# The last row blocks of a hybrid decoder layer: residual added ahead of a plain store, gates into tiles of their own, squares ahead of scalings

## The chip, the core and the metric

The kernel runs on one NeuronCore of a Trainium2 chip. Five engines work side by side, each with its own queue that it runs strictly in order: PE (TensorE) multiplies matrices into PSUM banks, DVE (VectorE) and ACT (ScalarE) work on tiles of 128 partitions, POOL (GpSimd) does the same more slowly and also issues DMAs, and SP (SyncE) issues DMAs. An instruction waits on semaphores of the instructions whose data it needs, and everything behind it in its queue waits with it. The metric is the device time of one execution in microseconds (us).

## The reference

One decoder layer on `x` of 1024 rows by 1024 columns in float32. Only its last line matters here:

```python
        h = rmsnorm(x, pre_w_mlp[l]) * (1.0 + sc2) + sh2
        u = jnp.square(jax.nn.relu(h @ w_up[l]))
        x = x + g2 * rmsnorm(u @ w_down[l], post_w_mlp[l])
    return x
```

So each row of the product `u @ w_down` is squared and summed over its 1024 columns, scaled by the inverse root of that mean, multiplied by `g2 * post_w_mlp` (in the kernel `gw2`, the gate), and added to the residual `x`.

## The kernel before

The output is cut into eight row blocks `tb` of 128 rows and two column halves of 512. The tile `accs[tb][half]` in SBUF, written (tb, half) below, gathers the product of the down projection. That projection is done by Strassen's scheme: seven products `n` instead of eight for each pair of row blocks t and t + 4, over five groups of the inner dimension (`GROUPS`). Each product of the last group (`g` = 4, two inner pairs `p`) is `dmm`: 2 x 3 matmuls of 128x128 by 512 columns, since every float32 operand is split into a high and a low part. Some products share a PSUM bank and go on summing in it, and `accum` on DVE adds the bank's running sum to a tile after each of them (`PLAN`): a, the bank of products 1, 6, 7 and 4; c, of 5 and 3; b, of 2. So within one bank each product has to wait until DVE has read the sum of the one before.

In the last group the order of work is a hand-written list of 24 steps (`order`, line 1586), three row pairs interleaved and the first three products of the fourth pair behind them. All five engine queues are pinned (class `Queue`): the instructions of each stand in exactly the order in which the code issues them. A step issues its matmuls, then the `accum` of the product of the step before, and then what the dictionary `later` holds for this step, in the order in which it was put there. The steps that matter, with the tile that each product is added to:

| step | product, bank | added to | step | product, bank | added to |
|---|---|---|---|---|---|
| 16 | 4, a of pair 1 | (5, 0) | 20 | 4, a of pair 2 | (6, 0) |
| 17 | 3, c of pair 2 | (2, 1) | 21 | 1, a of pair 3 | (3, 0) |
| 18 | 7, a of pair 2 | (6, 1) | 22 | 5, c of pair 3 | (7, 1) |
| 19 | 2, b of pair 2 | (2, 0) | 23 | 6, a of pair 3 | (3, 1) |

What follows a finished tile is made of six small functions: `square` (ACT squares it and sums the row into `ssr`), `gated` (DVE multiplies the tile by `gw2`, in place), `root` (a tiny DVE instruction adds the two sums, POOL raises to the power -1/2, giving `rr_`), `scaled` (ACT multiplies a half by `rr_`, in place), `onto_x` (POOL issues two accumulating DMAs that add the halves to `out`, which already holds the residual) and `store` (a plain DMA). For a finished second half at step s the code plans the gate and the root at s + 3, the two scalings at s + 4 and the DMAs at s + 5.

The residual comes from the middle of the kernel: `out_proj` writes it to `out`, but for the three halves in `hold` (line 1003), (3, 1), (7, 0) and (7, 1), to a DRAM buffer `x1d`. These three are loaded back by SP at the end of the list `seq` and added on DVE ahead of a plain store.

`last_rows` (line 1621) does the remaining products of pair 3: 2 into a fresh bank (`pdlb`), 3 into c, 7 into a, and 4 in two halves of 256 columns into a fresh bank (`pdlx`). Tile (7, 0) therefore gets two additions, of bank a and of `pdlx`. Its end: squares of the last pieces, the last root, one accumulating DMA of (3, 0) from POOL, and three plain stores of (3, 1), (7, 0) and (7, 1).

Of the kernel before, what the change touches and what calls it, by code (L numbers as in the profile page):

```python
# [47 lines left out]
def hybrid_layer(ctx: ExitStack, tc: tile.TileContext, I, out, dbg=None):  # L48
    nc = tc.nc
    ACT, DVE, POOL, PE, SP = (Queue(tc, e) for e in (nc.scalar, nc.vector, nc.gpsimd, nc.tensor, nc.sync))  # L50
# [21 lines left out]
    dram = ctx.enter_context(tc.tile_pool(name="dram", bufs=1, space=bass.MemoryType.DRAM))  # L72
# [7 lines left out]
    def m_(name, shape=(P, 512), dt=F32):  # L80
        return M.tile(list(shape), dt, tag="m", name=name)
# [554 lines left out]
    for tb in range(4):  # L636
        eng = DVE if tb < 2 else POOL
# [361 lines left out]

    x2ctx = ExitStack()  # L1000
    X2 = x2ctx.enter_context(tc.tile_pool(name="poolX2", bufs=1))
    x1d = dram.tile([P, 3 * 512], F32, tag="x1d", name="x1d")
    hold = {(3, 1): slice(0, 512), (7, 0): slice(512, D), (7, 1): slice(D, D + 512)}
    xn2 = [None] * TB

    def out_proj(tb):
# [264 lines left out]
    for i, (g, n) in enumerate(stages):  # L1271
# [3 lines left out]
        if 10 <= i and gates:  # L1275
            entry_gate(*gates.pop(0))
        ends.append(len(seq))
    for i in range(3):
        seq.append((f"x1_{i}", lambda i=i: x1d[:, i * 512:i * 512 + 512], None))

    def load_ahead():
        while at["load"] < min(len(seq), at["use"] + (LEAD if at["load"] >= 16 else 4) + 1):
            k = at["load"]
            mk = (raw_, t_)[k % 2] if k < 16 else (raw_, t_, t_, raw_, t_, raw_, t_, t_)[k % 8]
            rawt[k] = load_raw(mk, seq[k][0], seq[k][1]())
            at["load"] += 1

    def take():
        load_ahead()
        raw = rawt.pop(at["use"])  # L1290
        at["use"] += 1
        return raw

    def pump(count, limit=None):

        for _ in range(count):
            if at["use"] < (ends[-1] if limit is None else limit):
                k = at["use"]
                seq[k][2](take())
# [31 lines left out]
    gw2 = const.tile([P, D], F32, tag="gw1", name="gw2")  # L1331
# [130 lines left out]
    accs = [[None, None] for _ in range(TB)]  # L1462

    def dmm(pst, g, n, t, first, cols=slice(0, 512)):
        ps = GROUPS[g]
        for p in ps:
            (ah, al), (bh, bl) = (tuple(u[:, t * P:t * P + P] for u in su[p, n]), tuple(w[:, cols] for w in sw[p, n]))
            for x, (l, r) in enumerate(((ah, bh), (ah, bl), (al, bh))):
                PE.matmul(pst, lhsT=l, rhs=r, start=(first and p == ps[0] and x == 0), stop=(p == ps[-1] and x == 2),
                          skip_group_check=not first)  # L1470
# [81 lines left out]
    def store(tb, half, eng=None):  # L1552
        (eng or SP).dma_start(out[tb * P:(tb + 1) * P, half * 512:half * 512 + 512], accs[tb][half])

    ssr, rr_, later = {}, {}, {}

    def on(step, fn):
        later.setdefault(step, []).append(fn)

    def square(tb, half):  # L1560
        if tb not in ssr:
            ssr[tb] = small.tile([P, 2], F32, tag="ssf", name=f"ssf2{tb}")
        ACT.activation(a_ps(f"fin{tb}_{half}"), accs[tb][half], AF.Square, accum_out=ssr[tb][:, half:half + 1])

    def gated(tb, half):
        DVE.tensor_tensor(accs[tb][half], accs[tb][half], gw2[:, half * 512:half * 512 + 512], ALU.mult)

    def root_of(r, part, a, b):

# [3 lines left out]
    def root(tb):  # L1573
        ss, rr_[tb] = (small.tile([P, 1], F32, tag=f"{n}1", name=f"{n}f{tb}") for n in ("ss", "rr"))
        root_of(rr_[tb], ss, ssr[tb][:, 0:1], ssr[tb][:, 1:2])

    def scaled(tb, half):
        ACT.activation(accs[tb][half], accs[tb][half], AF.Copy, scale=rr_[tb][:, 0:1])

    def onto_x(tb, halves=(0, 1)):  # L1580

        for half in halves:
            POOL.dma_start(out[tb * P:(tb + 1) * P, half * 512:half * 512 + 512], accs[tb][half], accum_op=ALU.add)

    g = len(GROUPS) - 1
    order = sorted((7 * t + 2 * k, t, k) for t in range(3) for k in range(7))
    order += [(27 + k, 3, k) for k in range(3)]
    bk = {}
    for step, (_, t, k) in enumerate(order):
        n = ORDER[k]  # L1590
        key, first, th, half = PLAN[n]
        flush()
        if first:
            bk[key, t] = (mm_ps if key == "a" else tp_ps)(f"pd{key}{g}_{t}")
        dmm(bk[key, t], g, n, t, first)
        while todo:
            todo.pop(0)()
        todo.append(lambda tb=t + 4 * th, half=half, pst=bk[key, t]: accum(tb, half, pst))
        for fn in later.pop(step, []):
            fn()  # L1600
        if 2 <= step < 6:
            pump(1)
        if k >= 3 and t < 3:
            tb = t + 4 * th
            on(step + 1, lambda tb=tb, half=half: square(tb, half))
            if k < 5:
                on(step + 3, lambda tb=tb, half=half: gated(tb, half))
            else:
                on(step + 3, lambda tb=tb: root(tb))
                on(step + 3, lambda tb=tb, half=half: gated(tb, half))  # L1610
                for hf in (1 - half, half):
                    on(step + 4, lambda tb=tb, hf=hf: scaled(tb, hf))
                on(step + 5, lambda tb=tb: onto_x(tb))
    nstep = len(order)

    def rest(step):
        for fn in later.pop(step, []):
            fn()
        flush()

    def last_rows():
        a, b, t = 3, 7, 3
        ss = small.tile([P, 3], F32, tag="ssl", bufs=1, name="ssl")
        one = {n: small.tile([P, 1], F32, tag="l_" + n, bufs=1, name="l_" + n) for n in ("part", "r")}
        h = [slice(0, 512), slice(512, D)]
        ba, bc, bb, bx = bk["a", 3], bk["c", 3], tp_ps("pdlb"), tp_ps("pdlx")
        gl = [m_(f"gl{half}") for half in range(2)]
        ga0, ga = m_("ga0"), m_("ga")

        def sq(acc, col, w=512):  # L1630
            ACT.activation(a_ps("finl" + str(len(ssr)))[:, 0:w], acc, AF.Square, accum_out=col)

        def add(dst, pst):
            DVE.tensor_tensor(dst, pst, dst, ALU.add)

        dmm(bb, g, 2, t, True)
        while todo:
            todo.pop(0)()
        rest(nstep)
        dmm(bc, g, 3, t, False)  # L1640
        add(accs[a][0], bb)
        square(a, 0)
        rest(nstep + 1)
        dmm(ba, g, 7, t, False)
        add(accs[a][1], bc)
        square(a, 1)
        DVE.tensor_tensor(ga0, accs[a][0], gw2[:, h[0]], ALU.mult)
        DVE.tensor_tensor(ga, accs[a][1], gw2[:, h[1]], ALU.mult)
        rest(nstep + 2)
        acp = [accs[b][0][:, 256 * i:256 * i + 256] for i in range(2)]  # L1650
        dmm(bx[:, 0:256], g, 4, t, True, slice(0, 256))
        dmm(bx[:, 256:512], g, 4, t, True, slice(256, 512))
        for step in sorted(later):
            rest(step)
        add(accs[b][1], ba)
        sq(accs[b][1], ss[:, 0:1])
        root(a)
        add(accs[b][0], ba)
        for i in range(2):
            add(acp[i], bx[:, 256 * i:256 * i + 256])  # L1660
            sq(acp[i], ss[:, 1 + i:2 + i], 256)
        ACT.activation(ga0, ga0, AF.Copy, scale=rr_[a][:, 0:1])
        DVE.tensor_tensor(gl[1], accs[b][1], gw2[:, h[1]], ALU.mult)
        DVE.tensor_scalar(one["part"], ss[:, 0:1], ss[:, 1:2], D * EPS, ALU.add, ALU.add)
        DVE.tensor_tensor(one["part"], one["part"], ss[:, 2:3], ALU.add)
        POOL.tensor_tensor(one["r"], one["part"], mhalf[:, 0:1], ALU.pow)
        POOL.dma_start(out[a * P:(a + 1) * P, h[0]], ga0, accum_op=ALU.add)
        DVE.tensor_tensor(gl[0], accs[b][0], gw2[:, h[0]], ALU.mult)
        xa, xl = take(), [take() for _ in range(2)]
        DVE.scalar_tensor_tensor(ga, ga, rr_[a][:, 0:1], xa, ALU.mult, ALU.add)  # L1670
        nc.sync.dma_start(out[a * P:(a + 1) * P, h[1]], ga)
        for half in range(2):
            DVE.scalar_tensor_tensor(gl[half], gl[half], one["r"][:, 0:1], xl[half], ALU.mult, ALU.add)
            (nc.sync if half else nc.scalar).dma_start(out[b * P:(b + 1) * P, h[half]], gl[half])

    last_rows()


# [65 lines left out]
```

## Time and profile before

| what | value |
|---|---|
| median of 3 runs | 1100.62 us (1099.32 to 1101.92) |
| span of the profiled execution, first to last instruction | 1097.6 us |
| granted TensorE clock, mean | 0.996 |
| PE busy | 1076.2 us, 98% of the span |
| DVE, ACT, POOL busy | 795.1, 584.6 and 373.2 us |

The profiled execution's own device time isn't given beside its span; the median of the runs is 3.0 us over the span. In the profile every engine instruction that goes through a `Queue` has line 39, that of the helper, so groups are told apart by engine and by tile: `acc<-pda,acc` is an `accum` from a bank a, `acc<-acc,gw` a gate, `fin<-acc` a square (with an ACTIVATION_READ_ACCUMULATOR behind it that delivers the sum), `ssf<-ssf` the tiny addition of a root, `rrf<-ssf,mhalf` its power on POOL, `acc<-acc,rrf` a scaling, `out<-acc` a DMA of `onto_x`. A row of the timeline has its start, its duration, the engine, what it writes and reads, how often, and the idle time before it with what ended that. Line 1740 is the closing part that the program adds behind the kernel: each engine drains, SP waits for the last DMAs, and a barrier ends the span.

### The profile page before, as it was taken

The page shows a single profiled execution, that of the slowest core. Times are in us where ns is not written, and L with a number is a line of the kernel's source. Part 1 is how long each engine was busy: PE and PEld are TensorE (multiplying, and loading weights), DVE is VectorE, ACT ScalarE, POOL GpSimd, SP SyncE. Part 2 cuts the span into 40 slices and gives each one's busy share as a digit, 9 for nine tenths or more (in the row PEclk, how much of TensorE's full clock was granted, in tenths as well). Part 3 has the DMA queues.
Part 4 walks back from the last instruction along what each step waited for, and adds up shares of the span by engine and source line. Part 5 has one row for each costly group of instructions (what it writes and reads, how often), then busy time and mean ns, then how long its engine had stood idle before and what let it go on. Part 6 is the DMA issues. An engine that isn't in the chain of part 4 may idle for free.

```text
span 1097.6 us, 16208 instructions
## 1 busy us (share of the span) xinstructions
PE 1076.2 (98%) x5547; PEld 878.2 (80%) x5547; DVE 795.1 (72%) x1323; ACT 584.6 (53%) x1206; POOL 373.2 (34%) x499
## 2 busy tenths in 40 slices
PE   8999999999999999999999999999999999999995
PEld 6788776778888888888888888888888888888884
DVE  4365777878865574559776767876767787899876
ACT  3445544364565764566655555556664543555434
POOL 1153211033324663432543444533333333310014
PEclk9999999999999999999999999999999999999998
DMA  9701301534310352324577676767998888998537
GB/s 347 265 7 57 117 1 43 181 101 140 125 56 11 108 182 96 125 79 144 194 246 249 233 259 227 257 216 244 320 364 289 275 299 259 337 308 272 169 76 131
DMA packets 101587, 203.37 MB, mean 185 GB/s; under 512 B 13025, under 2 KB 13681, under 8 KB 101505
## 3 DMA queue, kind: packets, MB, share of 16 engines
q1 hardware_dynamic: 85968, 154.52, 41.4%
q0 software_dynamic: 15392, 47.57, 14.3%
q8 instruction: 43, 0.70, 0.3%
q14 instruction: 40, 0.32, 0.1%
q10 hardware_dynamic: 144, 0.26, 0.1%
HBM read 147.25 MB, written 55.05 MB: 184 GB/s over the span
## 4 chain that ended last, share of the span: by engine, by line
PE 92%; DVE 3%; ACT 1%; DMA 1%; POOL 1%; issue 1%; SPq 0%; DVEq 0%; POOLq 0%; ACTq 0%
PE pda L39 16%; PE pua L39 14%; PE pdc L39 8%; PE po L39 8%; PE puc L39 7%; PE pu L39 4%; PE pdb L39 4%; PE pq L39 4%; PE phg L39 4%; PE phq L39 3%; PE pub L39 3%; PE phf L39 3%; PE pv L39 3%; PE pk L39 2%; PE o L39 1%; PE sc L39 1%
## 5 line engine op out<-in xcount | busy, mean ns | idle before, releaser
L39 POOL TENSOR_TENSOR b<-b,b 128x512 f32<-128x512 f32 x64 | 89.6, 1400 | 222.8 <-DMA b<-w_dn 222.4
L39 ACT ACTIVATE dw<-dwr 128x512 fp32r<-128x512 f32 x72 | 45.4, 630 | 46.5 <-DMA dwr<-td 32.4
L39 ACT ACTIVATE s<-s 128x512 f32<-128x512 f32 x84 | 53.0, 631 | 31.8 <-DVE s L39 30.5
L39 DVE TENSOR_TENSOR dw<-dwr,dw 128x512 fp32r<-128x512 f32 x72 | 53.6, 744 | 9.0 <-ACT dw L39 8.9
L39 DVE TENSOR_TENSOR acc<-pda,acc 128x512 f32<-128x512 f32 x68 | 46.5, 684 | 13.7 <-PE pda L39 13.3
L39 POOL DMA_DIRECT2D td<-b x64 | 36.3, 567 | 21.6 <-POOL b L39 18.7
L39 POOL TENSOR_TENSOR rrf<-ssf,mhalf 128x1 f32<-128x1 f32 x7 | 7.9, 1253 | 95.3 <-DVE ssf L39 95.3
L39 DVE TENSOR_TENSOR wt<-s,wt 128x512 fp32r<-128x512 f32 x42 | 37.2, 886 | 2.6 <-ACT wt L39 2.5
L39 ACT ACTIVATE s<-pua 128x512 f32<-128x512 f32 x28 | 16.7, 598 | 39.4 <-PE pua L39 33.9
L39 ACT ACT_TABLE_LOAD x28 | 35.9, 1283 | 1.2 <-PEq L1737 0.7
L39 DVE SCALAR_TENSOR_TENSOR macc<-wada,cs,macc 128x512 f32<-128x512 f32 x42 | 33.7, 803 | 3.4 <-DMA wada<-wada 2.9
L39 POOL DMA_DIRECT2D b<-w_dn x64 | 34.4, 540 | 0.0
L39 POOL TENSOR_TENSOR comb<-comb,rd 128x512 f32<-128x512 f32 x8 | 11.7, 1458 | 63.3 <-DVE rd L39 44.2
L39 PE MATMUL pua<-bt_0h,wt 128*128 128x512 f32 x84 | 32.7, 389 | 0.0
L39 PE MATMUL pua<-bt_1h,wt 128*128 128x512 f32 x84 | 32.7, 389 | 0.0
L39 PE MATMUL pua<-bt_3h,wt 128*128 128x512 f32 x84 | 32.7, 389 | 0.0
L39 PE MATMUL pua<-bt_2h,wt 128*128 128x512 f32 x84 | 32.7, 389 | 0.0
L39 DVE TENSOR_TENSOR wt<-a,wt 128x512 fp32r<-128x512 f32 x42 | 31.0, 738 | 0.9 <-ACT wt L39 0.9
L39 DVE TENSOR_TENSOR acc<-pdc,acc 128x512 f32<-128x512 f32 x36 | 24.6, 684 | 8.5 <-PE pdc L39 8.4
L39 ACT ACTIVATE wt<-s 128x512 fp32r<-128x512 f32 x42 | 26.3, 626 | 8.2 <-DVE s L39 8.0
L39 PE MATMUL pda<-dw,du_6h 128*128 128x512 f32 x96 | 29.6, 389 | 0.0
L39 PE MATMUL pda<-dw,du_7h 128*128 128x512 f32 x96 | 29.5, 389 | 0.0
(757 smaller groups left out, 3746.1 us busy)
## 6 DMA issues: line engine op xcount, KB each, us to landing
dur<-ud SPq DMA_DIRECT2D x112, 256.0 KB, 4.5
wada<-wada SPq DMA_DIRECT2D x64, 256.0 KB, 3.5
b<-w_dn POOLq DMA_DIRECT2D x64, 256.0 KB, 5.2
td<-b POOLq DMA_DIRECT2D x64, 256.0 KB, 3.3
dwr<-td SPq DMA_DIRECT2D x64, 256.0 KB, 4.3
a<-w_u SPq DMA_DIRECT2D x56, 256.0 KB, 4.4
dwr<-w_dn SPq DMA_DIRECT2D x48, 256.0 KB, 4.5
ud<-s SPq DMA_DIRECT2D x42, 256.0 KB, 3.6
```

The lines of the kernel that those rows point to most:

```text
L39: ins = op(*args, **kw)
```

## The change

- `hold` grows from three halves to six: both halves of blocks 6, 3 and 7 go to `x1d` and come back by six loads of SP. They are taken at step 12.
- Block 6 and half (3, 0) lose their accumulating DMAs. A new function `with_x` multiplies by the root and adds the residual in one DVE instruction and stores from SP. (3, 1) is scaled on ACT, gets its residual on POOL, and is stored from SP.
- The gates of blocks 2, 3, 6 and 7 write new tiles, so that a gate and the square of the same tile no longer exclude each other. The two gates of block 3 go to POOL.
- In each step squares stand ahead of what else is planned for it, roots, scalings and DMAs move up by one or two steps.
- `last_rows` does the products in the order 2, 7, 3, 4, and 4 goes on in bank a; the fresh bank `pdlx` and one addition to (7, 0) go away.

```diff
-    x1d = dram.tile([P, 3 * 512], F32, tag="x1d", name="x1d")
-    hold = {(3, 1): slice(0, 512), (7, 0): slice(512, D), (7, 1): slice(D, D + 512)}
+    x1d = dram.tile([P, 6 * 512], F32, tag="x1d", name="x1d")
+    hold = {(tb, half): slice(1024 * i + 512 * half, 1024 * i + 512 * half + 512)
+            for i, tb in enumerate((6, 3, 7)) for half in range(2)}
...
-    for i in range(3):
+    for i in range(6):
         seq.append((f"x1_{i}", lambda i=i: x1d[:, i * 512:i * 512 + 512], None))
...
-    def on(step, fn):
-        later.setdefault(step, []).append(fn)
+    def on(step, fn, front=False):
+        fns = later.setdefault(step, [])
+        fns.insert(0 if front else len(fns), fn)
...
-    def gated(tb, half):
-        DVE.tensor_tensor(accs[tb][half], accs[tb][half], gw2[:, half * 512:half * 512 + 512], ALU.mult)
+    def gated(tb, half, eng=DVE):
+        acc = accs[tb][half]
+        if tb % 4 > 1:
+            accs[tb][half] = m_(f"gl{tb}_{half}")
+        eng.tensor_tensor(accs[tb][half], acc, gw2[:, half * 512:half * 512 + 512], ALU.mult)
...
+    def with_x(tb, half):
+        acc = accs[tb][half]
+        DVE.scalar_tensor_tensor(acc, acc, rr_[tb][:, 0:1], xt[tb, half], ALU.mult, ALU.add)
+        store(tb, half, nc.sync)
...
+        if step == 12:
+            xt = {(tb, half): take() for tb in (6, 3, 7) for half in range(2)}
         if k >= 3 and t < 3:
             tb = t + 4 * th
-            on(step + 1, lambda tb=tb, half=half: square(tb, half))
-            if k < 5:
+            on(step + 1, lambda tb=tb, half=half: square(tb, half), True)
+            if t == 2:
+                on(step + (4 if k == 4 else 2 if k == 3 else 1), lambda tb=tb, half=half: gated(tb, half))
+                if k == 5:
+                    on(step + 1, lambda tb=tb: root(tb))
+                elif k == 6:
+                    on(step + 2, lambda tb=tb: root(tb))
+                    for i, hf in enumerate((half, 1 - half)):
+                        on(step + 3 + i, lambda tb=tb, hf=hf: with_x(tb, hf))
+            elif k < 5:
                 on(step + 3, lambda tb=tb, half=half: gated(tb, half))
             else:
-                on(step + 3, lambda tb=tb: root(tb))
-                on(step + 3, lambda tb=tb, half=half: gated(tb, half))
+                on(step + 2, lambda tb=tb: root(tb))
+                on(step + 2, lambda tb=tb, half=half: gated(tb, half))
+            if k >= 5 and tb != 6:
                 for hf in (1 - half, half):
-                    on(step + 4, lambda tb=tb, hf=hf: scaled(tb, hf))
-                on(step + 5, lambda tb=tb: onto_x(tb))
+                    on(step + (2 if t == 2 else 3), lambda tb=tb, hf=hf: scaled(tb, hf))
+                on(step + (3 if t == 2 else 4), lambda tb=tb: onto_x(tb))
...
-        dmm(bc, g, 3, t, False)
+        dmm(ba, g, 7, t, False)
         add(accs[a][0], bb)
         square(a, 0)
+        gated(a, 0, POOL)
         rest(nstep + 1)
-        dmm(ba, g, 7, t, False)
+        dmm(bc, g, 3, t, False)
+        add(accs[b][1], ba)
+        sq(accs[b][1], ss[:, 0:1])
+        gated(b, 1)
+        rest(nstep + 2)
+        halves = [slice(0, 256), slice(256, 512)]
+        for c in halves:
+            dmm(ba[:, c], g, 4, t, False, c)
...
         add(accs[a][1], bc)
         square(a, 1)
...
+        gated(a, 1, POOL)
+        for i, c in enumerate(halves):
+            add(accs[b][0][:, c], ba[:, c])
+            sq(accs[b][0][:, c], ss[:, 1 + i:2 + i], 256)
         root(a)
...
+        gated(b, 0)
         DVE.tensor_scalar(one["part"], ss[:, 0:1], ss[:, 1:2], D * EPS, ALU.add, ALU.add)
         DVE.tensor_tensor(one["part"], one["part"], ss[:, 2:3], ALU.add)
         POOL.tensor_tensor(one["r"], one["part"], mhalf[:, 0:1], ALU.pow)
...
+        rr_[b] = one["r"]
+        scaled(a, 1)
+        with_x(a, 0)
+        POOL.tensor_tensor(accs[a][1], accs[a][1], xt[a, 1], ALU.add)
+        store(a, 1, nc.sync)
         for half in range(2):
...
+            acc = accs[b][half]
+            DVE.scalar_tensor_tensor(acc, acc, rr_[b][:, 0:1], xt[b, half], ALU.mult, ALU.add)
+            store(b, half, nc.sync if half else nc.scalar)
```

In `last_rows` a is block 3 and b block 7, `halves` are the two halves of 256 columns, `sq` a square into a sum of its own, and `rest(s)` runs what `later` holds for step s; `with_x` of (6, 1) stands at step 24, that is with the first product of `last_rows`.

More of the change, by code (lines that the diff above doesn't have):

```diff
@@ L1624, in last_rows @@
         one = {n: small.tile([P, 1], F32, tag="l_" + n, bufs=1, name="l_" + n) for n in ("part", "r")}
[L1625 to L1628, printed above, removed]
+        ba, bc, bb = bk["a", 3], bk["c", 3], tp_ps("pdlb")
         def sq(acc, col, w=512):
@@ L1639, in last_rows @@
         rest(nstep)
-        dmm(bc, g, 3, t, False)
+        dmm(ba, g, 7, t, False)
         add(accs[a][0], bb)
         square(a, 0)
+        gated(a, 0, POOL)
         rest(nstep + 1)
-        dmm(ba, g, 7, t, False)
+        dmm(bc, g, 3, t, False)
[6 more added lines that the diff above has]
+            dmm(ba[:, c], g, 4, t, False, c)
+        for step in sorted(later):
+            rest(step)
         add(accs[a][1], bc)
         square(a, 1)
[L1647 to L1656, printed above, removed]
-        root(a)
[L1658 to L1663, printed above, removed]
+        gated(a, 1, POOL)
+        for i, c in enumerate(halves):
+            add(accs[b][0][:, c], ba[:, c])
+            sq(accs[b][0][:, c], ss[:, 1 + i:2 + i], 256)
+        root(a)
+        gated(b, 0)
         DVE.tensor_scalar(one["part"], ss[:, 0:1], ss[:, 1:2], D * EPS, ALU.add, ALU.add)
@@ L1666, in last_rows @@
         POOL.tensor_tensor(one["r"], one["part"], mhalf[:, 0:1], ALU.pow)
[L1667 to L1671, printed above, removed]
+        rr_[b] = one["r"]
[3 more added lines that the diff above has]
+        store(a, 1, nc.sync)
         for half in range(2):
-            DVE.scalar_tensor_tensor(gl[half], gl[half], one["r"][:, 0:1], xl[half], ALU.mult, ALU.add)
-            (nc.sync if half else nc.scalar).dma_start(out[b * P:(b + 1) * P, h[half]], gl[half])
+            acc = accs[b][half]
+            DVE.scalar_tensor_tensor(acc, acc, rr_[b][:, 0:1], xt[b, half], ALU.mult, ALU.add)
+            store(b, half, nc.sync if half else nc.scalar)
     last_rows()
```

## The prediction, made before the change was run

> **What bounds the kernel now.** First the page's part 4, the chain that ended last, by engine.
>
> ```profile
> PE 92%; DVE 3%; ACT 1%; DMA 1%; POOL 1%; issue 1%; SPq 0%; DVEq 0%; POOLq 0%; ACTq 0%
> ```
>
> PE sets the time until its last matmul. An edit pays only behind that matmul; ahead of it, it can only cost, by making PE wait. Next, the chain in order of time, and the last matmul in the timeline:
>
> ```profile
> 1076.45 1.36 PE pdc L39 x6
> 1077.81 1.36 PE pda L39 x6
> 1079.17 1.36 PE pdlb L39 x6
> ```
> ```profile
> 1084.40 0.28 PE L39 MATMUL pdlx<-dw,du_4l 128*128 128x256 f32 x1
> ```
>
> The first three are steps 22 and 23 and product 2: 1.36 us each, no gap. PE ends at 1084.68. What lies between that and 1097.6? The timeline, the DMA issues, line 1740 and SP's waits answer:
>
> ```profile
> 1087.97 0.88 POOL L39 DMA_DIRECT2D out<-ga  x1
> ...
> 1089.62 0.34 SPq L1674 DMA_DIRECT2D out<-gl  x1
> ```
> ```profile
> out<-gl SPq DMA_DIRECT2D x1, 256.0 KB, 4.7
> ```
> ```profile
> L1740 POOLq DRAIN  x3: 46/99/9116, 1087.7 to 1097.3; - x3
> L1740 SPq DRAIN  x3: 7/7/7, 1094.5 to 1097.1; - x3
> ```
> ```profile
> SPq L1740 <- PEq L1740: 2.9, 2, 2.4
> SPq L1740 <- DMA out<-gl: 0.2, 1, 0.2
> ```
>
> The last store is issued at 1089.62 and lands 4.7 us later, at 1094.3. SP has seen it by 1094.58 (0.26 later) and then waits 2.4 us more. The view names PE, but PE had long been done: POOL's DRAIN began at 1087.7, took 9.116 us and ended at 1096.82. The span ends 0.78 us after that. POOL's last DMA was issued until 1088.85, so the DRAIN outlasted it by 8.0 us; the two DRAINs with no DMA out took 99 and 46 ns. I read it as waiting for POOL's DMAs. From the last store's issue to the end: 7.98 us.
>
> [...]
>
> **Part 1, the end.** The change takes away POOL's last DMAs: those of block 6 and of (3, 0). POOL's last DMA becomes the pair of (2, ·), over 8 us before POOL's last work. Then the end is: landing of the last store, 0.26, 0.78. For the landing, a plain SP store amid other traffic:
>
> ```profile
> ud<-s SPq DMA_DIRECT2D x42, 256.0 KB, 3.6
> ```
>
> Bounds are 3.6 and the 4.7 above, which shared the engines with accumulating DMAs; I take 4.0, nearer the first, since two other stores remain close before it. Sum 5.04 instead of 7.98: **−2.94 us** (−3.3 to −2.2).
>
> **Part 2, the first stall.** The root of block 2 moves from step 22 to step 20 on DVE, ahead of the `accum` of (6, 0), the new gate of (6, 0) and the `accum` of (3, 0). Here is DVE before, then ACT, then POOL:
>
> ```profile
> 1075.13 0.69 DVE L39 TENSOR_TENSOR acc<-pda,acc 128x512 f32<-128x512 f32 x1
> 1075.74 0.68 DVE L39 TENSOR_TENSOR acc<-acc,gw 128x512 f32<-128x512 f32 x1
> 1076.49 0.69 DVE L39 TENSOR_TENSOR acc<-pda,acc 128x512 f32<-128x512 f32 x1
> 1077.65 0.21 DVE L39 TENSOR_SCALAR ssf<-ssf 128x1 f32<-128x1 f32 x1 [0.47 <-ACT fin L39]
> 1077.78 0.68 DVE L39 TENSOR_TENSOR acc<-acc,gw 128x512 f32<-128x512 f32 x1
> ```
> ```profile
> 1071.01 0.19 ACT L39 ACTIVATION_READ_ACCUMULATOR fin<-acc 128x1 f32 x1
> 1071.56 1.34 ACT L39 ACTIVATE acc<-acc,rrf 128x512 f32<-128x512 f32 x2 [0.36 <-POOL rrf L39]
> ...
> 1075.59 1.34 ACT L39 ACTIVATE acc<-acc,rrf 128x512 f32<-128x512 f32 x2 [1.32 <-POOL rrf L39]
> 1076.83 0.58 ACT L39 ACTIVATE fin<-acc 128x512 f32<-128x512 f32 x1
> 1077.35 0.19 ACT L39 ACTIVATION_READ_ACCUMULATOR fin<-acc 128x1 f32 x1
> ```
> ```profile
> 1073.19 1.78 POOL L39 DMA_DIRECT2D out<-acc  x2 [1.67 <-ACT acc L39]
> 1074.48 1.07 POOL L39 TENSOR_TENSOR rrf<-ssf,mhalf 128x1 f32<-128x1 f32 x1
> ...
> 1077.23 1.79 POOL L39 DMA_DIRECT2D out<-acc  x2 [1.67 <-ACT acc L39]
> ```
>
> The square of (2, 0) delivers its sum at 1077.54, because it stands on ACT behind the two scalings of block 5. These wait for block 5's power on POOL, which stands behind block 1's two DMAs, and those wait for block 1's scalings. This order stays in the new code (steps 17 to 20). The whole chain can come forward only by as much as block 1's scalings can: from 1071.56 to the end of the square ahead of them, 1071.20 and 0.04, so by 0.32. Hence: DMAs at 1072.87, power done 1075.23, scalings 1075.27, square of (2, 0) delivered 1077.22.
>
> DVE stands idle until then. Root 1077.27, `accum` of (6, 0) 0.13 later (as in DVE's last two rows) at 1077.40, its gate 1078.18 (0.69 for the result it reads, 0.09 to hand over), `accum` of (3, 0) 0.60 later (the pitch of DVE's first two rows) at 1078.78, done 1079.47, where before it began at 1076.49. It reads bank a, in which step 23 goes on summing: PE starts that at 1079.54 instead of 1077.81. **+1.73 us** (2.0 if the chain doesn't come forward; 0.4 if it came a whole step forward).
>
> **Part 3, the second stall.** On DVE `with_x` of (6, 0) now stands ahead of the `accum` of (3, 1), which product 7 in bank a waits for. It needs block 6's power, behind block 2's DMAs on POOL. By the spacings above: scalings of 5 at 1075.27, DMAs 1.64 later at 1076.91 to 1078.70, block 2's power 0.58 (as 1075.55 stands to 1074.97 above) to 1079.28, scalings 1079.32, DMAs 1080.96 to 1082.75, block 6's power to 1083.33. `with_x` starts at 1083.39; of such operations two take 1.41 (last row of part 4), so one holds its engine for about 0.66, and the `accum` runs from 1084.05 to 1084.74. Product 7 starts at 1084.81; with the first stall alone it would start at 1082.26. **+2.55 us.** Each hand-over in it may be off by 0.1; over six of them that is 0.6 on either side. The last matmul then ends at 1084.68 + 4.28 = 1088.96.
>
> **Part 4, from the last matmul to the last store.**
>
> ```profile
> 1085.25 0.76 DVE L39 TENSOR_TENSOR acc<-pdlx,acc 128x256 f32<-128x256 f32 x2
> 1086.63 0.18 ACT L39 ACTIVATION_READ_ACCUMULATOR finl<-acc 128x1 f32 x1
> 1086.85 0.16 DVE L39 TENSOR_TENSOR l_part<-l_part,ssl 128x1 f32<-128x1 f32 x1
> 1087.08 0.93 POOL L39 TENSOR_TENSOR l_r<-l_part,mhalf 128x1 f32<-128x1 f32 x1 [1.08 <-DVE l_part L39]
> 1088.19 1.41 DVE L39 SCALAR_TENSOR_TENSOR gl<-gl,l_r,x 128x512 f32<-128x512 f32 x2
> ```
>
> Before, the last addition ended 1.33 after PE's end, since the full addition of bank a to (7, 0) stood ahead of it; the last sum came at +2.13, the power at +3.33, the store at +4.94. Now that addition is gone, but other work stands ahead, and POOL's gates get in DVE's way, as the next rows show:
>
> ```profile
> 223.51 1.29 POOL L39 TENSOR_TENSOR k<-k,k 128x512 f32<-128x512 f32 x1
> ...
> 223.57 1.78 DVE L39 TENSOR_TENSOR whf1l<-whf1r,whf1h 128x512 fp32r<-128x512 f32 x1
> ```
>
> A DVE operation that reads two SBUF tiles, 0.68 alone (the gate rows above), ended 0.55 after POOL's operation. So DVE's gate of (7, 1) ends 0.55 after POOL's gate of (3, 0), and the addition to (3, 1) starts some 1.1 ahead of PE's end. Its square ends at about +0.4, the two squares of 256 columns, half a us each, at +1.5. POOL gates (3, 1) from −0.3 to +1.0, does block 3's power to +1.55; DVE's gate of (7, 0) ends 0.55 after POOL's gate, the two tiny additions at +1.9, the last power at +3.0. So 0.3 is won here. Then POOL adds the residual to (3, 1) while DVE does the two last operations, which read two SBUF tiles each. By the same rows: POOL's addition 1.3, the first DVE operation 0.55 after it, the second 0.66 later, issue 0.03: the last store at +5.54, **+0.60 us**. If DVE got in first, (3, 1) would be stored after both and (7, 1) behind it on SP, some 0.9 later; without this effect, 0.6 earlier.
>
> **At nothing:** three more loads of SP, covered by 30 us of matmuls:
>
> ```profile
> 1043.28 2.12 SPq L39 DMA_DIRECT2D x<-x1d  x3
> ```
>
> Nothing but stores stands behind them on SP; without that cover each would cost a landing. The larger `x1d` moves no more bytes in `out_proj`. Steps 0 to 19 stay on time: a gate or an `accum`, 0.6 each, fit twice in 1.36.
>
> **Sum:** 1.73 + 2.55 + 0.60 − 2.94 = +1.94 on the span, 1099.5; on the median 1100.62, with the same 3.0 around the span, **1102.5 us**. With the bounds of its terms this case reaches from 1101.3 to 1104.0.
>
> **Rivals.**
>
> *PE doesn't wait* (12%). Then only parts 1 and 4 count: +0.60 − 2.94 = −2.3, 1098.3. For it: before, no step was late. Against: DVE's rows stand in program order, and the sum at 1077.54 is a measured time. The chain would have to be 1.7 us shorter.
>
> *One stall only* (8%): block 6's power comes early enough, 1100.0.
>
> *The DRAIN counts from POOL's last work, not from its DMAs* (14%), the slow one. POOL's last addition ends at 1093.2; 8.0 later it is 1101.2, and with 0.78 the span ends at 1102.0: +4.4, 1105.0. It decides once the DRAIN outlasts that addition by 5.6 us, since SP's list is done at 1098.8. For it: only one long DRAIN exists here, and it can't be told what it counts from. Against: the short ones.
>
> *PE's clock drops in the second stall* (5%).
>
> ```profile
> 1084.68:1088.60 3.92, 0.00 (x1) 0.00 (x0) 3.69 (x9) 2.19 (x7) 2.84 (x4) 1.00 1.07 152
> 1088.60:1097.60 9.00, 0.00 (x0) 0.00 (x0) 0.99 (x2) 0.00 (x0) 0.26 (x1) 0.50 0.59 145
> ```
>
> The granted clock held at 1.00 for 3.9 us after the last matmul and was 0.50 behind that. If 2.55 us were enough, the last 4.2 us of matmuls would take twice as long: 1106.7. [...]
>
> **How the numbers follow.** The forecast has 61%. A measurement of this kernel can tell about 0.2% (2.2 us) from no change: under 1098.4 is faster, over 1102.8 slower. Of the forecast's 61%, 26 lie over 1102.8 (its middle is 0.3 under it) and 34 within; 1 is left for faster. The DRAIN and the clock (19) are slower. One stall (8) is within. Of the 12 without stalls 9 are faster. Slower 0.45, same 0.45, faster 0.10. The range 1098.4 to 1105.2 leaves out the clock, most of the case without stalls and a little of the DRAIN.
>
> **What would show it.** Step 23 about 1.7 us and product 7 about 4.3 us late, with DVE waiting for an ACT square and then for a power; if both start on time, parts 2 and 3 are wrong. POOL's DRAIN under 1 us, SP's last wait ending on a DMA; a DRAIN of 8 us means the slow rival. One of the last two DVE operations at 1.7 us instead of 0.74; if both take 0.74, part 4 is 0.6 or more too dear.

## The result, and the profile after

The changed kernel takes 1104.18 us (median of 6 runs, 1101.76 to 1105.91) against 1100.19 (1099.32 to 1101.92) for the kernel before on the same chip: ratio 1.0036 [1.0024, 1.0048], slower by 4 us. The profiled execution took 1104.07 us with a span of 1102.2.

First PE and DVE of the changed kernel, from the timeline (start, duration, engine, operation, and in brackets the idle time ahead of it with what ended it). These rows stand against steps 22 and 23 and product 2 of the prediction's first fences, which ran without a gap.

```profile
1079.58 0.73 PE L39 MATMUL pda<-dw,du_6h 128*128 128x512 f32 x2 [2.05 <-DVE acc L39]
1084.83 0.73 PE L39 MATMUL pda<-dw,du_7h 128*128 128x512 f32 x2 [2.23 <-DVE acc L39]
...
1090.58 0.28 PE L39 MATMUL pda<-dw,du_4l 128*128 128x256 f32 x1
```
```profile
1077.39 0.21 DVE L39 TENSOR_SCALAR ssf<-ssf 128x1 f32<-128x1 f32 x1 [2.48 <-ACT fin L39]
...
1078.85 0.68 DVE L39 TENSOR_TENSOR acc<-pda,acc 128x512 f32<-128x512 f32 x1
...
1083.43 0.75 DVE L39 SCALAR_TENSOR_TENSOR gl<-gl,rrf,x 128x512 f32<-128x512 f32 x1 [2.58 <-POOL rrf L39]
1084.10 0.68 DVE L39 TENSOR_TENSOR acc<-pda,acc 128x512 f32<-128x512 f32 x1
```

PE waits twice. The first row of DVE is the root of block 2, held 2.48 us by an ACT square; the `accum` that step 23 needs comes two operations later. The row at 1083.43 is `with_x` of (6, 0), held 2.58 us by a power; the `accum` behind it lets product 7 start. PE ends at 1090.86 instead of 1084.68.

The stalls alone don't make these 6.2 us. The view by stretches has, for each, PE's busy time in its second column, and after the five engines the granted clock. The stretches follow the clock's own changes: it fell to 0.50 at 1085.95, was back at 1.00 at 1089.36, 3.41 us later, and fell again at 1092.78, 3.42 later; the other rows step back from there by the same length. That the clock is set by windows of this length, one behind the other, is a reading of these distances.

```profile
1075.71:1079.13 3.42, 1.82 (x9) 1.17 (x7) 1.70 (x4) 2.30 (x6) 2.16 (x3) 1.00 0.80 98
1082.54:1085.95 3.41, 1.18 (x6) 0.94 (x6) 2.52 (x4) 0.00 (x0) 0.85 (x2) 1.00 1.04 150
1085.95:1089.36 3.41, 3.41 (x10) 2.63 (x9) 1.47 (x3) 1.45 (x4) 1.28 (x1) 0.50 0.44 157
1089.36:1092.78 3.42, 1.50 (x13) 1.30 (x11) 2.45 (x7) 1.74 (x6) 2.14 (x2) 1.00 0.00 0
```

In the second row PE is busy for 1.18 of 3.41 us, and in the third it runs at half speed: product 3 takes 2.56 us there (1086.64 to 1089.20), where a product took 1.36 in the prediction's first fences. In the fourth it is busy for 1.50 of 3.42 us, and the clock is 0.50 again from 1092.78, where PE has had nothing left to do for 1.92 us. From product 7's start to PE's end the kernel now takes 6.03 us (1084.83 to 1090.86); the same three products took 4.31 before, from this row of the kernel before's timeline to its end at 1084.68:

```profile
1080.37 0.62 PE L39 MATMUL pdc<-dw,du_3h 128*128 128x512 f32 x2
```

That is 1.72 us more, nearly all of it lost clock (e5 below gives 1.54).

Then the end: the last DVE row, POOL's last DMAs and its last operation, the closing part's line (1758 now, 1740 before; the shortest, the median and the longest of its DRAINs in ns), SP's waits, and the landing.

```profile
1093.50 2.41 DVE L39 SCALAR_TENSOR_TENSOR gl<-gl,l_r,x 128x512 f32<-128x512 f32 x2
```
```profile
1081.02 1.79 POOL L39 DMA_DIRECT2D out<-gl  x2 [1.67 <-ACT gl L39]
...
1093.62 1.74 POOL L39 TENSOR_TENSOR gl<-gl,x 128x512 f32<-128x512 f32 x1 [0.23 <-ACT gl L39]
```
```profile
L1758 POOLq DRAIN  x3: 46/99/7821, 1093.6 to 1101.9; - x3
L1758 SPq DRAIN  x3: 7/7/7, 1098.4 to 1101.7; - x3
```
```profile
SPq L1758 <- PEq L1758: 3.7, 2, 3.2
SPq L1758 <- DMA out<-gl: 1.5, 2, 1.0
```
```profile
out<-gl SPq DMA_DIRECT2D x5, 256.0 KB, 2.1
```

The last store is issued at 1095.93, and SP has done its list at 1098.42: the last landing took 2.1 us instead of 4.7. But POOL's DRAIN still takes 7.8 us and ends at 1101.41, though POOL's last DMA was issued by 1082.81 (1081.02 + 1.79). It ends 6.05 us after POOL's last addition (1093.62 + 1.74). DVE's closing DRAIN, by contrast, ends 0.05 us after DVE's last operation (1095.96 and 1095.91).

| piece of the span (us) | before | predicted | after |
|---|---|---|---|
| PE's last matmul ends | 1084.68 | 1088.96 | 1090.86 |
| from there to the last store's issue | 4.94 | 5.54 | 5.07 |
| from there to the end | 7.98 | 5.04 | 6.27 |
| span | 1097.6 | 1099.5 | 1102.2 |

### The profile page after: what moved, and what is told of

Same layout as the page of the kernel before. It is cut to its first block, busy times and chain, and to the rows that moved or that the text cites. A ratio compares the mean times of both kernels' runs of the same rounds, so it can differ in the third digit from the quotient of the medians.

```text
span 1102.2 us, 16216 instructions
## 1 busy us (share of the span) xinstructions
PE 1078.7 (98%) x5547; PEld 879.2 (80%) x5547; DVE 788.3 (72%) x1322; ACT 583.5 (53%) x1204; POOL 372.3 (34%) x499
## 4 chain that ended last, share of the span: by engine, by line
PE 91%; DVE 3%; POOL 2%; ACT 2%; issue 1%; DMA 1%; SPq 0%; DVEq 0%; POOLq 0%; ACTq 0%
PE pda L39 15%; PE pua L39 14%; PE pdc L39 8%; PE po L39 8%; PE puc L39 7%; PE pu L39 4%; PE pq L39 4%; PE pdb L39 4%; PE phg L39 4%; PE phq L39 3%; PE pub L39 3%; PE phf L39 3%; PE pv L39 3%; PE pk L39 2%; PE o L39 1%; PE sc L39 1%
## 5 line engine op out<-in xcount | busy, mean ns | idle before, releaser
L39 DVE TENSOR_TENSOR acc<-pda,acc 128x512 f32<-128x512 f32 (+1 forms) x69 | 46.5, 676 | 15.6 <-PE pda L39 15.5
L39 DVE TENSOR_TENSOR s<-puc,s 128x512 f32<-128x512 f32 x14 | 9.7, 690 | 30.9 <-issue 28.4
```

Source lines behind the costliest of these rows:

```text
L39: ins = op(*args, **kw)
```

## Experiments

All are compared with the kernel before on the same chip; its median was 1099.74 in the first eight runs and 1099.78 in the last.

**e1 and e2: each stall alone.** The first undoes the early root of block 2, the second moves `with_x` of block 6 behind the additions that PE waits for.

```diff
 e1
-                    on(step + 1, lambda tb=tb: root(tb))
+                    on(step + 3, lambda tb=tb: root(tb))
...
-                    on(step + (2 if t == 2 else 3), lambda tb=tb, hf=hf: scaled(tb, hf))
+                    on(step + 3, lambda tb=tb, hf=hf: scaled(tb, hf))
 e2
-                    for i, hf in enumerate((half, 1 - half)):
-                        on(step + 3 + i, lambda tb=tb, hf=hf: with_x(tb, hf))
...
         gated(b, 1)
+        with_x(6, 0)
+        with_x(6, 1)
         rest(nstep + 2)
```

> The changed kernel with one edit: block 2's root goes back behind the additions and gates of steps 21 and 22 on DVE, so the first stall goes; the order on POOL stays (block 5's DMAs, power of 2, DMAs of 2, power of 6). Theory: the second stall is set by POOL's chain alone, so step 23 starts on time (about 1.7 to 2 us earlier than in the changed kernel) but product 7 starts at the same 1084.8 us, behind one gap of some 4 us; the granted clock falls again, and the median is that of the changed kernel, 1104.2 +- 1. Rival, two stalls that add up: 1.7 to 2 us are saved, 1102.3.

> The changed kernel with one edit: the two operations that scale block 6 and add its residual stand on DVE behind the gate of (7, 1) instead of around the addition to (3, 1). Theory: the second stall goes, product 7 starts 1.7 to 2 us late instead of 4.3, the clock stays at 1.00, and 2.5 + 1.7 us are saved: 1100.0. If the clock's fall has nothing to do with the second gap, it comes again and only 2.5 are saved: 1101.7.

e1 took 1104.54 us (1.0044 [1.0029, 1.0059]), e2 1102.62 (1.0025 [1.0013, 1.0036]). PE in e1, then in e2, and e2's stretches on its own grid:

```profile
1084.71 1.18 PE L39 MATMUL pda<-dw,du_7h 128*128 128x512 f32 x2 [4.57 <-DVE acc L39]
```
```profile
1079.72 0.74 PE L39 MATMUL pda<-dw,du_6h 128*128 128x512 f32 x2 [2.05 <-DVE acc L39]
```
```profile
1077.74:1081.15 3.41, 1.43 (x6) 1.19 (x7) 3.21 (x7) 2.06 (x4) 1.74 (x4) 1.00 0.87 114
1081.15:1084.56 3.41, 3.41 (x10) 2.67 (x9) 1.16 (x2) 0.00 (x0) 2.36 (x3) 0.50 0.87 124
```

In e1 the first wait is gone and the second is 4.57 instead of 2.23: product 7 starts when it did (1084.71 against 1084.83), since what it waits for, block 6's power behind block 2's DMAs on POOL, hasn't moved. Taken away alone, the first stall is worth nothing. In e2 one wait of 2.05 us is left, and the clock fell behind it all the same: 1.98 us of the wait lay in one window, in which PE was busy for 1.43 of 3.41 us. In the changed kernel the same wait of 2.05 us is split by a window's edge at 1079.13 into 1.60 and 0.45, and the clock stayed at 1.00. e2 missed both of its values (1100.0 and 1101.7): PE ends 2.35 us earlier than in the changed kernel (1088.51), but POOL's last addition only 1.38 us earlier (1093.98), and the span falls by no more than that (1102.2 to 1100.8).

**e3: both edits together.**

> The changed kernel with both edits. Theory: PE never waits in the last group, its last matmul ends where it did before (1084.4 to 1084.7 us), the clock stays at 1.00, and the whole 6.2 us by which PE was late are saved, less up to 0.5 for block 6's late operations on DVE: 1098.0 to 1098.5, faster than before. Rival, that the change costs by contention of POOL and DVE or by its DMAs: PE's end stays late, over 1101. POOL's DRAIN: if it counts from POOL's last work it ends about 6 us after that; if it waits for POOL's DMAs it is over before SP's last wait.

1101.02 us (1.0013 [1.0004, 1.0022]), 2.5 us over what was expected. PE has no wait and ends at 1084.38. What took its place is in the tail (DVE, then POOL):

```profile
1082.36 2.81 DVE L39 TENSOR_TENSOR gl<-acc,gw 128x512 f32<-128x512 f32 x1
1085.09 1.40 DVE L39 SCALAR_TENSOR_TENSOR gl<-gl,rrf,x 128x512 f32<-128x512 f32 x2
...
1090.11 2.41 DVE L39 SCALAR_TENSOR_TENSOR gl<-gl,l_r,x 128x512 f32<-128x512 f32 x2
```
```profile
1082.68 1.93 POOL L39 TENSOR_TENSOR gl<-acc,gw 128x512 f32<-128x512 f32 x1
```
```profile
1082.67:1086.09 3.42, 1.71 (x14) 1.47 (x12) 3.42 (x3) 0.47 (x2) 1.94 (x3) 1.00 0.93 141
1086.09:1089.50 3.41, 0.00 (x0) 0.00 (x0) 3.07 (x9) 1.81 (x7) 2.26 (x3) 1.00 0.41 156
```

DVE's gate of (7, 1) takes 2.81 us: it ends at 1085.17, 0.56 after POOL's gate (1082.68 + 1.93). With PE early, DVE was late, and the last store came 8.2 us behind PE's end. What ends the span is POOL's DRAIN again, at 1098.02, 6.05 us after POOL's last addition; SP's list was done at 1095.05. The stretches give a second bound for the clock: PE busy for half of a window (1.71 of 3.42), and no drop in the next.

**e4: the kernel before with one edit.** Only half (3, 0) changes its way out: a fourth half in `x1d`, the residual on DVE, a plain store.

```diff
...
-        ACT.activation(ga0, ga0, AF.Copy, scale=rr_[a][:, 0:1])
...
-        POOL.dma_start(out[a * P:(a + 1) * P, h[0]], ga0, accum_op=ALU.add)
...
-        xa, xl = take(), [take() for _ in range(2)]
+        xa, xl, x0 = take(), [take() for _ in range(2)], take()
+        DVE.scalar_tensor_tensor(ga0, ga0, rr_[a][:, 0:1], x0, ALU.mult, ALU.add)
+        nc.sync.dma_start(out[a * P:(a + 1) * P, h[0]], ga0)
```

> The kernel before with one edit: half (3, 0) gets its residual on DVE and a plain store of SP, so POOL's last work is the last power (end about 1088.0 us) instead of an accumulating DMA. PE's end stays at 1084.7. Theory, DRAIN lasts 6 us from POOL's last work and some 2 more behind a DMA: it ends at 1094.0, SP's last store sets the end, -2.2 to -2.8 us on the span, 1097.5 to 1098. Rival, 8 us from POOL's last work whatever that is: DRAIN ends at 1096.0, -0.8 us, 1099.4. Rival, it takes its time from something else than POOL's work: 1100.2, no change.

1097.64 us (0.9986 [0.9976, 0.9995]): 2.1 us under the kernel before, the interval just clear of no change. So a plain store in place of the last accumulating DMA pays by itself, with nothing else of the change. The DRAIN still takes 7.4 us. It ends at 1094.91, 6.4 after POOL's last power and 0.9 later than expected, and so 0.4 after SP's list was done (1094.51).

```profile
1087.54 0.93 POOL L39 TENSOR_TENSOR l_r<-l_part,mhalf 128x1 f32<-128x1 f32 x1 [1.09 <-DVE l_part L39]
```
```profile
L1740 POOLq DRAIN  x3: 46/99/7412, 1087.5 to 1095.4; - x3
```

**e5: the clock alone.** The changed kernel with matmuls that nobody reads in PE's two waits.

```diff
+        if step == 22:
+            fill = tp_ps("fill")
+            for i in range(7):
+                PE.matmul(fill, lhsT=su[15, 6][0][:, 0:P], rhs=sw[15, 6][0], start=True, stop=True)
...
         dmm(bb, g, 2, t, True)
+        for i in range(8):
+            PE.matmul(fill, lhsT=su[15, 6][0][:, 0:P], rhs=sw[15, 6][0], start=True, stop=True)
```

> The changed kernel with 15 extra matmuls into a bank that nobody reads, 7 behind step 22's product and 8 behind product 2, so that TensorE is busy in its two waits; nothing else differs, and the fillers' results are used nowhere. Theory (the clock fell to 0.50 because TensorE stood idle for more than half of one 3.41 us window, and that cost the 1.7 to 1.9 us that the two stalls alone don't explain): the granted clock stays 1.00 until the last product, products 7 and 3 start where they did (1084.8), their matmuls take 0.34 each again, TensorE ends at 1089.0 instead of 1090.86, and the run is at 1102.2 to 1102.6 (1.7 under the changed kernel). Rival (the clock falls for another reason, by time or by load): TensorE ends at 1090.9 and the run stays at 1104.2. Second rival (the fillers themselves delay product 3's group by queueing): up to 0.3 more.

1103.14 us (1.0029 [1.0019, 1.0040]); the profiled span is 1100.7.

```profile
1079.62 0.73 PE L39 MATMUL pda<-dw,du_6h 128*128 128x512 f32 x2 [0.47 <-DVE acc L39]
1084.87 0.73 PE L39 MATMUL pda<-dw,du_7h 128*128 128x512 f32 x2 [0.42 <-DVE acc L39]
```
```profile
1085.95:1089.36 3.41, 3.37 (x21) 2.84 (x19) 2.15 (x5) 2.10 (x6) 1.96 (x2) 1.00 0.55 175
```

Both products start within 0.04 of the changed kernel's, with the fillers ahead of them; the clock stays at 1.00, a single matmul of 512 columns in products 7 and 3 takes 0.39 to 0.40 us (the expectation had 0.34), where it took 0.63 at the clock of 0.50 in the changed kernel, and PE ends at 1089.32 instead of 1090.86. The windows of this run have another phase (the clock falls at 1092.29, behind PE's last matmul), but the second wait lies whole in one of them too: from 1082.05 to 1085.46 PE is busy for 2.99 us, nearly two thirds of it in the fillers (1.97). So the drop follows PE's idleness and costs 1.54 us of span. The medians differ by 1.0, less than was expected, and their intervals overlap; the spans and the clock's rows carry this conclusion.

**e6: GpSimd's big operations off the tail.** e3 with block 3's gates and the residual of (3, 1) on DVE.

```diff
-        gated(a, 0, POOL)
+        gated(a, 0)
...
-        gated(a, 1, POOL)
+        gated(a, 1)
...
-        scaled(a, 1)
         with_x(a, 0)
-        POOL.tensor_tensor(accs[a][1], accs[a][1], xt[a, 1], ALU.add)
-        store(a, 1, nc.sync)
+        with_x(a, 1)
```

> Experiment e3 (both moves late, no wait of TensorE) with block 3's two gates and the residual of its half (3,1) on VectorE instead of GpSimd, so that GpSimd has no 512-wide operation left at the end. Theory (in e3 the tail was 8.2 us long behind TensorE's end because VectorE's gate of (7,1) was held to 2.81 us by GpSimd's gate and its last two operations to 2.41 by GpSimd's addition, and GpSimd's closing DRAIN ends 6.0 to 6.4 us after GpSimd's last operation): the gate of (7,1) takes 0.68, the last two together 1.4, last store 5 to 6 us behind TensorE's end, the DRAIN ends 6.4 us after the last power, span 1096.0 to 1097.0, time 1098.2 to 1099.4 (1.6 to 2.8 under e3). Rival (those operations are no longer on VectorE than on GpSimd, VectorE being the engine with the most to do at the end): three more operations of 0.7 on VectorE give back 2.1 us, and it stays at 1101.0.

1098.19 us (0.9985 [0.9976, 0.9994]), 2.8 under e3, at the theory's bound.

```profile
1082.36 0.69 DVE L39 TENSOR_TENSOR gl<-acc,gw 128x512 f32<-128x512 f32 x1
...
1089.65 1.41 DVE L39 SCALAR_TENSOR_TENSOR gl<-gl,l_r,x 128x512 f32<-128x512 f32 x2
```

The same gate takes 0.69 instead of 2.81, the same last pair 1.41 instead of 2.41. The store comes 6.7 us behind PE's end, though, not 5 to 6: DVE has more to do now. The gain itself is the DRAIN's: the last store is issued 1.46 us earlier than in e3 (1091.09 and 1092.55), the span 3.34 us shorter, and POOL's last work ends 3.34 us earlier (1088.63 and 1091.97).

**e7: the DRAIN alone.** e4 with one unread operation of one column more on POOL, behind all others.

```diff
+        spare = small.tile([P, 1], F32, tag="l_s", bufs=1, name="l_s")
+        POOL.tensor_tensor(spare, gl[1][:, 0:1], mhalf[:, 0:1], ALU.add)
```

> Experiment e4 with one more operation of one column on GpSimd, reading the last tile after VectorE has made it (its result is used nowhere); stores and all else as in e4. Theory (GpSimd's closing DRAIN ends a fixed 6.0 to 6.4 us after GpSimd's last operation): the operation ends at about 1091.2 instead of the power's 1088.5, the DRAIN at 1097.4 instead of 1094.9, and the time rises by 2.2 to 2.8 to about 1100.1. Rival (the DRAIN follows from the stores' landing, or from the end of the program on the other engines): the DRAIN ends within 0.4 of e4's, and the time is within 0.5 of e4's 1097.6.

1099.76 us (0.9996 [0.9987, 1.0006]): 2.1 over e4, for an operation of 0.19 us that nothing waits for.

```profile
1091.31 0.19 POOL L39 TENSOR_TENSOR l_s<-gl,mhalf 128x1 f32<-128x1 f32 x1 [2.32 <-DVE gl L39]
```
```profile
L1742 POOLq DRAIN  x3: 46/108/6437, 1091.3 to 1098.2; - x3
```

The DRAIN ends 6.2 us after it, at 1097.7, where e4's ended at 1094.9. Of these 2.8 us 0.5 are the whole trace's (PE ends at 1085.65 instead of 1085.13); the stores stand to PE's end as they did. So the DRAIN's end goes with POOL's last work, even where that is one column.

**e8 and e9: what follows from it.** e8 keeps the plain stores for blocks 6 and 3, has block 6's power ahead of block 2's DMAs on POOL, and spreads `with_x` and the gates between the additions. e9 takes the last two roots off POOL as well. e8's lines stand against e6, e9's against e8.

```diff
 e8
-                on(step + (3 if t == 2 else 4), lambda tb=tb: onto_x(tb))
+                on(step + 4, lambda tb=tb: onto_x(tb))
...
         dmm(ba, g, 7, t, False)
+        with_x(6, 0)
         add(accs[a][0], bb)
         square(a, 0)
-        gated(a, 0)
+        with_x(6, 1)
...
         sq(accs[b][1], ss[:, 0:1])
+        gated(a, 0)
         gated(b, 1)
-        with_x(6, 0)
-        with_x(6, 1)
 e9
...
+        ACT.activation(wr, rr_[2], AF.Sqrt)
         dmm(ba, g, 7, t, False)
...
-        root(a)
...
+        DVE.tensor_scalar(pa, ssr[a][:, 0:1], ssr[a][:, 1:2], D * EPS, ALU.add, ALU.add)
+        DVE.reciprocal(inv[0], pa)
         gated(b, 0)
+        ACT.activation(rr_[a], inv[0], AF.Sqrt)
...
-        POOL.tensor_tensor(one["r"], one["part"], mhalf[:, 0:1], ALU.pow)
+        DVE.reciprocal(inv[1], one["part"])
+        ACT.activation(one["r"], inv[1], AF.Sqrt)
```

> What the theory makes of the change: residuals of blocks 6 and 3 added on VectorE ahead of plain stores as in the change, but block 2's root stays behind block 6's additions (no first wait), block 6's power is ahead of block 2's DMAs on GpSimd (no second wait: the power doesn't queue behind them), block 6's additions of x stand between the products' additions, and GpSimd has no 512-wide operation at the end. Theory: TensorE never waits and ends at 1084.4, granted clock 1.00, last power ends 3.3 behind TensorE's end at 1087.7, last store 4.6 behind it at 1089.0, DRAIN ends at 1094.1, span 1094.9, time 1096.9 (2.8 under the kernel before, 0.7 under e4). Rival (VectorE, which has all gates and residuals now, is what ends last): last store 6 to 7 behind TensorE's end, time 1098.2 to 1099.0.

> Experiment e8 with the last two roots (blocks 3 and 7) taken off GpSimd: VectorE's reciprocal and ScalarE's square root in place of GpSimd's power, with one square root of one column, unread, ahead of product 7 so that ScalarE's table is loaded before it is needed. GpSimd's last work is then the issue of block 2's two accumulating DMAs, which ended at 1083.9 in e8. Theory (the DRAIN follows GpSimd's own last work, not the stores of SP): it ends 8.0 us after that issue as in the kernel before, at 1091.8, or earlier; SP's last landing (1093.4 in e8) then sets the end, span 1094.2, time 1095.9, which is 2.0 under e8. Rival (the DRAIN ends some 4 us behind the last store whatever GpSimd did): no change, 1097.9. Second rival (the roots on two engines are dearer than one power): the last store up to 0.6 later, time 1096.5.

e8 took 1097.9 us (0.9981 [0.9972, 0.9990]), 1.0 over its expectation and level with e4 and e6. No wait of PE, no drop ahead of its last matmul; but PE ended at 1085.48 instead of 1084.4, since the whole end of this trace lies 1.1 us later than e3's, the last power ended 3.9 us behind PE's end, not 3.3, and the DRAIN 6.05 after that. e9 took 1095.62 (0.9958 [0.9944, 0.9972]): 4.2 us under the kernel before, and the fastest of all. POOL's last work and its DRAIN in e9, SP's waits, and ACT's table:

```profile
1081.60 1.79 POOL L39 DMA_DIRECT2D out<-gl  x2 [1.16 <-ACT gl L39]
```
```profile
L1764 POOLq DRAIN  x3: 46/108/9302, 1082.0 to 1093.4; - x3
```
```profile
SPq L1764 <- DMA out<-gl: 1.5, 3, 0.7
SPq L1764 <- PEq L1764: 0.7, 2, 0.5
```
```profile
1081.32 1.28 ACT L39 ACT_TABLE_LOAD   x1
1082.62 0.20 ACT L39 ACTIVATE l_w<-rrf 128x1 f32<-128x1 f32 x1
```

The DRAIN is the longest of all, 9.3 us, and hurts nobody: it began at 1082.0 and ended at 1091.32, 7.9 after POOL's last DMA issue. SP's list was done at 1092.92, and the wait behind it that the view puts down to PE is 0.5, where the changed kernel had 3.2. Each new root costs two short operations (0.16 us on DVE and 0.19 to 0.20 on ACT) instead of one power (0.88 and 1.02 in e8), and the last store stands 5.47 us behind PE's end as in e8. The load of the square root's table, 1.28 us, put the first of ACT's last squares off by 0.8 us against e8; the third was on time again (both less the 0.5 us by which e8's trace lies later).

Put together, from each trace (us): the end of POOL's last operation other than a DMA, the landing of its last accumulating DMA, and the DRAIN's end, with its distance from both.

| kernel | POOL's last operation ends | its last DMA lands | DRAIN ends | after the operation | after the landing |
|---|---|---|---|---|---|
| before | power, 1088.01 | 1093.67 | 1096.82 | 8.80 | 3.15 |
| changed | addition of 512 columns, 1095.36 | 1086.96 | 1101.41 | 6.05 | 14.45 |
| e1 | the same, 1095.23 | 1087.23 | 1101.28 | 6.05 | 14.05 |
| e2 | the same, 1093.98 | 1087.19 | 1100.03 | 6.05 | 12.84 |
| e3 | the same, 1091.97 | 1086.67 | 1098.02 | 6.05 | 11.35 |
| e4 | power, 1088.47 | 1091.80 | 1094.91 | 6.45 | 3.11 |
| e5 | addition of 512 columns, 1093.82 | 1087.32 | 1099.86 | 6.05 | 12.54 |
| e6 | power, 1088.63 | 1086.50 | 1094.68 | 6.05 | 8.18 |
| e7 | addition of 1 column, 1091.50 | 1092.69 | 1097.71 | 6.21 | 5.02 |
| e8 | power, 1089.34 | 1088.68 | 1095.39 | 6.05 | 6.71 |
| e9 | power, 1080.44 | 1088.29 | 1091.32 | 10.88 | 3.03 |

One reading fits all eleven rows within 0.2 us: the DRAIN ends 6.05 us after POOL's last operation or 3.1 us after the landing of its last accumulating DMA, whichever is later. The landing decides in the kernel before, in e4 and in e9, the operation in the others. The first half is shown, by e7 above all. The second half is not: in the kernel before and in e9 the DRAIN's end is also 7.96 and 7.93 us from the end of the last DMA's issue (1088.86 and 1083.39), and only e4 speaks for the landing, where that issue ended at 1085.87 and 7.95 later would be 1093.82, and 6.05 after the power 1094.52, for 1094.91 measured. No run was made to tell the two apart.

## Why the prediction was right or wrong

**Parts 2 and 3, the stalls, were right**, mechanism and time. Step 23 was to start at 1079.54 and did at 1079.58; product 7 at 1084.81, and did at 1084.83. The root waited for the square, and `with_x` for the power, as worked out from the order on each queue. What the prediction didn't see is that its two terms are not two prices: e1 removed the first and won nothing, because the second wait is set by POOL's chain alone, wherever PE stands.

**Part 1, the end, failed at its reading of the DRAIN.** The step took POOL's DRAIN to wait for POOL's DMAs and for nothing else ("I read it as waiting for POOL's DMAs"), so that with these out of the way early it would be under 1 us. What it lacked is that an operation of POOL alone holds the DRAIN's end for 6.05 to 6.21 us, as e7 and the table show; in the changed kernel that was POOL's last addition, which the change itself put there. As to the kernel before, the reading may stand: there the DRAIN ended with the last DMA, be it 3.1 us from the landing or 8.0 us from the issue. The other term of the step erred to the good: the last store was to land in 4.0 us, with 3.6 as the lower bound, and landed in 2.1. SP's list was done 2.5 us after the last store (1095.93 to 1098.42), earlier than the forecast's 4.26; the DRAIN ended 3.0 later and took it back. Measured −1.7 instead of −2.94. The rival that had 14% was right in kind. Its span of 1102.0 nearly met the measured 1102.2 by two errors: 8.0 instead of 6.05 for the DRAIN, and POOL's last addition at 1093.2 where it ended at 1095.36.

**The clock, left out of the forecast, was the other error.** The prediction asked whether 2.55 us in one piece were enough, and took the 3.9 us behind the last matmul for a bound. That row doesn't give one: counted back from the fall at 1088.60, 0.5 of the 3.9 us were the rest of a window in which PE had been busy and 3.41 a whole idle one, and in the changed kernel the clock fell 1.92 us behind the last matmul (1090.86 to 1092.78). The rows of the changed kernel, e2 and e3 go with the share of a 3.41 us window: PE idle for 47% of one (changed kernel) or for 50% (e3) kept the clock, for 56% (changed kernel, its last window), 58% (e2) or 65% (changed kernel) lost it. Where between 50% and 56% the limit lies is open. With PE kept busy in both waits (e5) the clock stayed at 1.00. The rival's price of 4.2 was too high, because the clock came back after 3.41 us (1085.95 to 1089.36): 1.54 by e5. A wholly idle window was not needed: the clock fell behind windows in which PE had been busy for 42% (e2) and 44% (changed kernel).

**PE's end** was thus 1.90 us later than forecast (1090.86 for 1088.96). 1.54 of it is the clock; the other 0.36 shows in e5 too, where PE ends at 1089.32. The sum was short there: it gave the last three products 4.15 us from product 7's start (1084.81 to 1088.96), and with a full clock they take 4.45 (e5, 1084.87 to 1089.32).

**Part 4, the tail, was right in mechanism and 0.47 too dear.** The last pair on DVE took 2.41 us instead of 1.41 beside POOL's addition, and e6 shows both this and the gate's 2.81 gone with POOL's operations. The last power ended 2.54 us behind PE's end, where the sum had 3.0. The loads, put at nothing, cost nothing: the six of them ran from 1042.99 to 1052.00, and PE's first wait in the last group is the one at step 23.

**The time around the span** was mis-sized too. The prediction carried 3.0 us over from the median of before. The profiled execution of the changed kernel has 1.9 (1104.07 less 1102.2), and all 61 runs of the kernel before beside the experiments have 1.7 to 1.8 between time and span. So the profiled execution of before, with a span of 1097.6, took about 1099.4, and not the median of 1100.62. On the span the forecast was 2.7 us low (1099.5 for 1102.2), on the median only 1.7: that it came so near is partly luck, for the 1.1 us too much around the span made up for part of the 2.7 too little in it.

## What to carry to other kernels

A queue's last work can be a term of the end, even where nobody reads its result: in e7 one unread operation of 0.19 us on POOL put the end off by 2.1 us. Give the engine whose closing drain is long (POOL here, 6.4 to 9.3 us) its last work, DMAs included, early; e4, without the last accumulating DMA, won 2.1 us. Before moving an operation ahead of what TensorE waits for, follow what it itself waits for through every queue, and test two stalls together, since removing the first alone may only lengthen the second (2.23 us became 4.57 in e1). A short wait of TensorE can cost its length and the clock behind it: here the wait of 2.23 us was followed by 3.41 us at 0.50, worth 1.54 by e5.

## What the runs showed that was not expected

- POOL's closing DRAIN was long in every kernel (6.4 to 9.3 us) and ended 6.05 to 6.21 us after POOL's last operation, unless its last accumulating DMA was late (three traces): then it ended 3.03 to 3.15 us after the landing. Why it takes that long wasn't tried. SP's closing DRAINs took 7 ns (the kernel before, the changed one, e3 to e9).
- The granted clock fell to 0.50 behind windows of 3.41 us in which PE was idle for 56% (changed kernel), 58% (e2) and 65% (changed kernel), and not behind one of 50% (e3); where PE was busy again it was back at 1.00 after 3.41 us. One and the same wait of 2.05 us kept the clock where a window's edge split it and lost it where it lay in one window. The windows' phase differs from trace to trace (edges at 1085.95 in the changed kernel, 1084.56 in e2, 1086.09 in e3), which may add to the spread of the changed kernel's runs, 4.2 us; but those of the kernel before spread over 1.3 to 3.7, and this wasn't tested.
- The changed kernel's last three stores from SP, 256 KB each, with nothing but another plain store under way, landed in 2.0 to 2.1 us, its two in the time of block 2's accumulating DMAs in 2.8 and 3.4; the last one of the kernel before, amid accumulating DMAs, in 4.7.
